# State-space layer on one Trainium2 core: the reads of its outputs move from the SP queue to the POOL queue

## The chip, the cores and the metric

The kernel runs on one core of one Trainium2 chip. The metric is device time in microseconds (us), the median of several executions; lower is better. The engines are TensorE (PE; its weight loads are listed as PEld), VectorE (DVE), ScalarE (ACT), GpSimd (POOL) and SyncE (SP). Each works through its own list of instructions in order, and waits on semaphores for the others and for transfers (DMAs). SP does nothing but issue DMAs. POOL issues DMAs too, and clears tiles between them.

## The reference, cut to what matters

The whole is a model of two blocks. The second block begins with a state-space layer, `s5_mixer`, on a sequence of 1024 positions and 1024 channels (64 groups of 16 channels, 64 states each):

```
bu_re = jnp.einsum('blgh,gph->lbgp', u, bb_re)
bu_im = jnp.einsum('blgh,gph->lbgp', u, bb_im)
_, _, s_re, s_im = lax.associative_scan(
    _ssm_combine, (a_seq_re, a_seq_im, bu_re, bu_im), axis=0)
y = (jnp.einsum('lbgp,ghp->blgh', s_re, c_re.astype(f32))
     - jnp.einsum('lbgp,ghp->blgh', s_im, c_im.astype(f32)))
y = y.reshape(bsz, seq, D_MODEL) + d_skip.astype(f32) * x.astype(f32)
h = jax.nn.gelu(y).astype(x.dtype)
val, gate = jnp.split(h @ w_glu, 2, axis=-1)
z = val * jax.nn.sigmoid(gate)
return (z @ w_out).astype(x.dtype)
```

## The kernel before

`block2` calls `s5_main`, which works in eight batches b = 0 to 7 of 128 channels (8 groups). The sequence is cut into 128 chunks of 8 positions. For one batch there are these steps, each a function inside `s5_main` or called by it:

- `s5_load(b)` and `u_tile(b)`: SP loads the tables E, ph, D and Co of the batch (five DMAs of 256 to 512 KB, L1476 and L1482) and the inputs U (eight DMAs of 64 KB, L1491). POOL first clears half of each of the two Co tiles (L1481).
- `states(b)`: PE multiplies U by E (tiles pe_re and pe_im, 32 matmuls, L1505). DVE turns the products by ph, scans over the chunks and turns back (L1247 to L1252 inside `cmul`, L1513); the result is S.
- `outputs(b)`: 48 matmuls on PE (tiles py, L1531 to L1533) from U, D, S and Co; ACT copies them to Y (L1534), and POOL writes Y to the scratch tensor y_d in HBM (tile name s5y, L1535, 512 KB).
- `tail(b)`: y_d is read back in another order, as eight DMAs of 64 KB (tile s5yt, L1544; one for each position within a chunk). ACT applies gelu (L1547) and casts the result (L215), DVE subtracts for the low halves (L216, tile s5hl, two of them).
- `glu(b)`: 12 matmuls on PE of s5hl with the first two weight panels (tile pg, L202 to L204).

The loop interleaves the batches:

```
for b in range(8):
    states(b)
    if b >= 1:
        outputs(b - 1)
        if b + 1 < 8:
            self.s5_load(b + 1)
            self.u_tile(b + 1)
    if b >= 3:
        tail(b - 3)
    if b >= 4:
        glu(b - 4)
```

After it come outputs(7), tail(5), glu(4), tail(6), and then glu(5) to glu(7) with the matmuls of two more panels (glu1, tile pg1) and tail(7) among them. The code's order is not the executed one: when the program is built, a scheduler of the tile framework sets the order of instructions on each engine, from its own estimate of when each is ready. So an edit of one line can change the order on engines that the line does not name. The order on every engine, once built, is fixed.

All tiles of 4 KB per partition share one pool of 40 buffers, so a load can have to wait until an older tile is no longer read. A DMA's completion is told on one of eight semaphores for the DMAs of SP and ACT, and one of eight others for those of POOL, taken in turn; a DMA waits for the one that used its semaphore before.

Of the kernel before, what the change touches and what calls it, by code (L numbers as in the profile page):

```python
# [103 lines left out]
class Core:  # L104
# [1388 lines left out]
    def s5_main(self):  # L1493
        nc, d = self.nc, self.d
        y_d = self.scr("s5y", [8, 8, 16, 8, P])
# [45 lines left out]
        def tail(b):  # L1541
            yt = self.t("s5yt", (P, 8, P))
            for t in range(8):
                nc.sync.dma_start(yt[:, t], y_d[b, t].rearrange("h g c -> g h c"))  # L1544
            yt = yt.rearrange("p s c -> p (s c)")
            y = self.t("s5y")
            nc.scalar.activation(y.rearrange("p (c s) -> p s c", s=8)[:, ::-1, ::-1],  # L1547
                                 yt.rearrange("p (s c) -> p s c", s=8), AF.Gelu_apprx_tanh)
            for hv, q in zip(HALVES, hs):
                hl = self.tr("s5hl", (P, 2, HB))  # L1550
                self.split(y[:, hv], hl[:, 0], hl[:, 1])
                q.append((hl[:, 0], hl[:, 1]))
            ys.append(y)
# [7 lines left out]
# [11 lines that stand above are left out]
        outputs(7)  # L1572
        tail(5)
        glu(4)
        tail(6)
        w1 = [self.weights(d["w_glu"][i], [P, KT, P], True) for i in (9, 1)]
        p1 = [self.psb("pg1") for _ in range(4)]
# [659 lines left out]
```

## Time and profile before

| what | value |
|---|---|
| median of 3 runs | 4070.12 us (4068.89 to 4072.51) |
| the profiled execution, its own time | 4067.31 us |
| its span, first to last instruction | 4065.5 us |
| PE busy, whole span | 3800.5 us (93%) |
| DVE busy | 2841.9 us (70%) |
| ACT busy | 1445.5 us (36%) |
| POOL busy | 308.7 us (8%) |
| granted TensorE clock, mean | 0.967 of full |

The page gives busy time by engine over the span, and the share says nothing of a single stage. Times in the answers of the trace count from the start of the span. The state-space layer's loop lies between about 1587 and 1707 us; the rows below are from there.

### The profile page before, as it was taken

To read this page: it belongs to the slowest core of one execution; us is meant where nothing else is said; L and a number is where in the kernel's file an instruction comes from. 1 tells how busy PE (TensorE), PEld (TensorE's weight loads), DVE (VectorE), ACT (ScalarE), POOL (GpSimd) and SP (SyncE) were. 2 spreads that over 40 slices of the span, in tenths; PEclk is the share of its full clock that TensorE was granted. 3 is DMA by queue.
4 is the path that set the end of the run, shared out by engine and by line. 5 is a ranking of instruction groups with operands and counts; after the bars stand their busy time and mean duration, and the time that the engine had idled before them with its cause. 6 is when DMAs were issued, how large, how long until landed. Compare 5 with 4: busy or idle time off the path is not lost.

```text
span 4065.5 us, 51267 instructions
## 1 busy us (share of the span) xinstructions
PE 3800.5 (93%) x19684; PEld 3145.8 (77%) x19684; DVE 2841.9 (70%) x4892; ACT 1445.5 (36%) x2328; POOL 308.7 (8%) x533
## 2 busy tenths in 40 slices
PE   7899899899999997799999999989999899999998
PEld 4778788778788866687788888878787677888886
DVE  5676767786888778667866664458878867666545
ACT  3222245533111221433423333335555634332332
POOL 0001100041010022000000000011010000000000
PEclk8999999999999998999999999989999899999999
DMA  6433321063222248513322245323232332122443
GB/s 235 138 113 128 111 77 42 28 212 130 73 73 74 98 148 253 164 53 103 125 80 76 94 153 171 122 83 99 73 99 73 89 124 109 73 94 78 170 159 111
DMA packets 172907, 458.35 MB, mean 113 GB/s; under 512 B 38542, under 2 KB 59028, under 8 KB 172662
## 3 DMA queue, kind: packets, MB, share of 16 engines
q1 hardware_dynamic: 129254, 317.94, 23.8%
q0 software_dynamic: 41104, 132.41, 9.9%
q10 hardware_dynamic: 2304, 4.72, 0.3%
q8 instruction: 155, 2.54, 0.3%
q14 instruction: 90, 0.74, 0.1%
HBM read 327.07 MB, written 100.66 MB: 105 GB/s over the span
## 4 chain that ended last, share of the span: by engine, by line
PE 75%; DVE 13%; issue 4%; DMA 3%; ACT 3%; POOL 1%; SPq 0%; POOLq 0%; DVEq 0%; ACTq 0%
PE p L202 7%; PE p L203 7%; PE p L204 7%; PE pd L202 4%; PE pd L204 4%; PE pd L203 4%; PE pout L202 2%; PE pout L204 2%; PE pout L203 2%; DVE sbm L1964 2%; PE pu L202 2%; PE pu L204 2%; PE pu L203 2%; PE pwt L1985 1%; PE pz L1047 1%
## 5 line engine op out<-in xcount | busy, mean ns | idle before, releaser
L185 DVE TENSOR_TENSOR wl<-wt,wh 128x1024 fp32r<-128x1024 f32 x232 | 283.3, 1222 | 276.5 <-ACT wh L184 274.1
L184 ACT CAST wh<-wt 128x1024 fp32r<-128x1024 f32 x232 | 242.9, 1048 | 653.5 <-PE pd L203 189.9
L202 PE MATMUL p<-tq,wq 128*128 128x512 f32 x736 | 290.5, 395 | 3.6 <-ACT wq L215 3.6
L203 PE MATMUL p<-tq,wq 128*128 128x512 f32 x736 | 290.0, 394 | 0.0
L204 PE MATMUL p<-tq,wq 128*128 128x512 f32 x736 | 290.0, 394 | 0.0
L202 PE MATMUL pd<-hd,wh 128*128 128x512 f32 x704 | 277.7, 394 | 2.8 <-DVE r L1831 2.8
L204 PE MATMUL pd<-hd,wl 128*128 128x512 f32 x704 | 276.5, 393 | 0.0
L203 PE MATMUL pd<-hd,wh 128*128 128x512 f32 x704 | 276.3, 393 | 0.0
L203 PE MATMUL p<-hq,wq 128*128 128x512 f32 x480 | 189.7, 395 | 0.0
L202 PE MATMUL p<-hq,wq 128*128 128x512 f32 x480 | 189.4, 395 | 0.0
L204 PE MATMUL p<-hq,wq 128*128 128x512 f32 x480 | 189.0, 394 | 0.0
L215 ACT CAST wq<-ws 128x512 fp32r<-128x512 f32 x184 | 114.3, 622 | 208.7 <-PE p L204 204.0
L1723 DVE TENSOR_TENSOR fsg<-fsg,p 128x512 f32<-128x512 f32 x140 | 94.4, 686 | 117.1 <-PE p L204 117.1
L202 PEld LDWEIGHTS p<-tq,wq 128*128 128x128 f32 x736 | 138.1, 188 | 43.3 <-ACT wq L215 4.9
L204 PEld LDWEIGHTS p<-tq,wq 128*128 128x128 f32 x736 | 138.3, 188 | 32.2
L203 PEld LDWEIGHTS p<-tq,wq 128*128 128x128 f32 x736 | 138.2, 188 | 30.6
L1723 DVE TENSOR_TENSOR fsu<-fsu,p 128x512 f32<-128x512 f32 x140 | 94.5, 687 | 93.7 <-PE p L204 93.6
L216 DVE TENSOR_TENSOR wq<-ws,wq 128x512 fp32r<-128x512 f32 x184 | 126.7, 690 | 46.4 <-ACT wq L215 44.5
L202 PEld LDWEIGHTS pd<-hd,wh 128*128 128x128 f32 x704 | 132.2, 188 | 33.9 <-DVE r L1831 4.2
L204 PEld LDWEIGHTS pd<-hd,wl 128*128 128x128 f32 x704 | 132.2, 188 | 31.2 <-DVE wl L185 0.6
L203 PEld LDWEIGHTS pd<-hd,wh 128*128 128x128 f32 x704 | 132.2, 188 | 30.0
L202 PE MATMUL pu<-hq,wh 128*128 128x512 f32 x320 | 129.8, 406 | 9.5 <-DVE cv L984 9.5
(702 smaller groups left out, 10657.4 us busy)
## 6 DMA issues: line engine op xcount, KB each, us to landing
wt<-w_gu SPq DMA_DIRECT2D x88, 512.0 KB
wt<-w_dn SPq DMA_DIRECT2D x88, 512.0 KB
wm<-w_mod SPq DMA_DIRECT2D x48, 512.0 KB
hid<-fsg POOLq DMA_DIRECT2D x44, 512.0 KB, 3.9
hr<-hid SPq DMA_DIRECT2D x44, 512.0 KB
wt<-w_od SPq DMA_DIRECT2D x28, 512.0 KB
khat<-fX POOLq DMA_DIRECT2D x24, 512.0 KB, 3.0
kh<-khat SPq DMA_DIRECT2D x24, 512.0 KB
```

Source lines behind the costliest of these rows:

```text
L184: nc.scalar.copy(wh, wt)
L185: nc.vector.tensor_tensor(wl, wt, wh.bitcast(F32), op=ALU.subtract)
L202: mm(ps, lh, rh, start=first, stop=False)
L203: mm(ps, lh, rl, start=False, stop=False)
L204: mm(ps, ll, rh, start=False, stop=last)
L215: self.nc.scalar.copy(h, src)
L216: self.nc.vector.tensor_tensor(l, src, h.bitcast(F32), op=ALU.subtract)
L1047: mm(p4[:, i, q], tb[:, m], z[:, self.POS[m]], start=True, stop=False)
L1723: add = lambda o, u, v: tt(o, u, v, op=ALU.add)
L1964: nc.vector.tensor_tensor_scan(om[:, :n - 1], om[:, :n - 1], self.inv[:, 3:4].to_broadcast([P, n - 1]), 1.0, op0=ALU.mult, op1=ALU.add)
L1985: nc.tensor.transpose(pt[:, s * P:(s + 1) * P], W[x][:, c:c + P], self.ident)
```

## The change

The eight DMAs of `tail` that read y_d back are issued by POOL instead of SP:

```diff
         def tail(b):
             yt = self.t("s5yt", (P, 8, P))
             for t in range(8):
-                nc.sync.dma_start(yt[:, t], y_d[b, t].rearrange("h g c -> g h c"))
+                nc.gpsimd.dma_start(yt[:, t], y_d[b, t].rearrange("h g c -> g h c"))
             yt = yt.rearrange("p s c -> p (s c)")
             y = self.t("s5y")
```

That is 64 DMAs in all. With it the built order changes on all engines. On SP the tail's reads are gone from between the loads. Before, where the inputs U of batch 4 have been issued (s5U_13155):

```order
L1491 DMA s5U_13155<-xf_d_11866 16x8x128 x8
L1544 DMA s5yt_13164<-s5y_12828 128x1x128 x8
L1476 DMA s5E_13253<-s5e_6947 128x1024
L1476 DMA s5ph_13255<-s5p_6949 128x1024
L1476 DMA s5D_13257<-s5m_6951 128x1024
```

and now:

```order
L1491 DMA s5U_13155<-xf_d_11866 16x8x128 x8
L1476 DMA s5E_13253<-s5e_6947 128x1024
L1476 DMA s5ph_13255<-s5p_6949 128x1024
L1476 DMA s5D_13257<-s5m_6951 128x1024
L1482 DMA s5Co_13259<-s5c_6948 64x1024
```

The loads of batch 5 (s5E_13253 and on) follow those of batch 4 at once.

On POOL the reads stand behind the write of a later batch. Tail 0 is s5yt_13164 and tail 1 is s5yt_13274; the Y tiles of batches 2, 3 and 4 are s5Y_13113, s5Y_13223 and s5Y_13345. Before:

```order
L1535 DMA s5y_12828<-s5Y_13113 128x1024
L1481 MEMSET s5Co_13152 64x1024
L1516 MEMSET s5S_13215 128x8
L1535 DMA s5y_12828<-s5Y_13223 128x1024
L1481 MEMSET s5Co_13259 64x1024
L1481 MEMSET s5Co_13262 64x1024
L1516 MEMSET s5S_13337 128x8
L1535 DMA s5y_12828<-s5Y_13345 128x1024
```

and now:

```order
L1535 DMA s5y_12828<-s5Y_13113 128x1024
L1481 MEMSET s5Co_13152 64x1024
L1544 DMA s5yt_13164<-s5y_12828 128x1x128 x8
L1516 MEMSET s5S_13215 128x8
L1481 MEMSET s5Co_13259 64x1024
L1535 DMA s5y_12828<-s5Y_13223 128x1024
L1481 MEMSET s5Co_13262 64x1024
L1544 DMA s5yt_13274<-s5y_12828 128x1x128 x8
L1516 MEMSET s5S_13337 128x8
```

So tail 1 is issued after the write of batch 3, and the same pattern goes on: tail k after the write of batch k + 2, up to tail 3.

On PE the twelve matmuls of glu 0 (tile pg0, from s5hl_13175 and s5hl_13178) move. Before, between the last matmul of batch 2's outputs (py5_13128) and the first of batch 3's (py5_13224), there stood only the states' products of batch 4:

```order
L1533 MATMUL py5_13128<-s5S_13012,s5Co_12966 128x128
L1505 MATMUL pe_re_13181<-s5U_13155,s5E_13143 64x128 x8
L1505 MATMUL pe_im_13182<-s5U_13155,s5E_13143 64x128 x8
L1531 MATMUL py5_13224<-s5U_13062,s5D_13054 128x128
L1532 MATMUL py5_13224<-s5S_13105,s5Co_13056 128x128
```

and now, at the same place, glu 0 comes first (its first rows):

```order
L1533 MATMUL py5_13128<-s5S_13012,s5Co_12966 128x128
L202 MATMUL pg0_12841<-s5hl_13175,wh_12831 128x512
L203 MATMUL pg0_12841<-s5hl_13175,wh_12831 128x512
L204 MATMUL pg0_12841<-s5hl_13175,wl_12832 128x512
L202 MATMUL pg0_12841<-s5hl_13178,wh_12831 128x512
```

and its last row is followed by what was next to py5_13128 before:

```order
L203 MATMUL pg0_12842<-s5hl_13178,wh_12837 128x512
L204 MATMUL pg0_12842<-s5hl_13178,wl_12838 128x512
L1505 MATMUL pe_re_13181<-s5U_13155,s5E_13143 64x128 x8
L1505 MATMUL pe_im_13182<-s5U_13155,s5E_13143 64x128 x8
L1531 MATMUL py5_13224<-s5U_13062,s5D_13054 128x128
```

Before, glu k stood behind the outputs of batch k + 3; now it stands ahead of the states' products of batch k + 4 and of those outputs. This holds for k = 0 to 3. Behind batch 7's outputs the order of PE is nearly the same as it was: glu 4, glu 5, then glu 6 and glu1.

## Rows read from the trace of the kernel before

**Rows 1.** The page, part 1: busy us, share of span, instructions.

```profile
PE 3800.5 (93%) x19684; PEld 3145.8 (77%) x19684; DVE 2841.9 (70%) x4892; ACT 1445.5 (36%) x2328; POOL 308.7 (8%) x533
```

**Rows 2.** Busy time by stretch, all engines; stretch, length, busy by engine, clock, DMA.

```profile
core 0: us, PE busy (x) PEld busy (x) DVE busy (x) ACT busy (x) POOL busy (x), PEclk, DMA share, GB/s
...
1630.00:1650.00 20.00, 14.60 (x126) 12.41 (x126) 11.17 (x23) 5.49 (x6) 2.48 (x4) 0.91 0.76 216
...
1690.00:1710.00 20.00, 13.24 (x74) 10.91 (x73) 11.10 (x22) 8.51 (x10) 0.53 (x1) 0.91 0.28 89
1710.00:1730.00 20.00, 20.00 (x88) 15.95 (x87) 17.73 (x28) 12.91 (x20) 0.00 (x0) 1.00 0.27 80
```

**Rows 3.** SP's queue in time: start, length, what, count.

```profile
1627.63 5.64 SPq L1544 DMA_DIRECT2D s5yt<-s5y  x8
...
1636.13 8.40 SPq L1491 DMA_DIRECT2D s5U<-xf_d  x8
1644.70 4.93 SPq L1544 DMA_DIRECT2D s5yt<-s5y  x8
...
1660.78 4.93 SPq L1544 DMA_DIRECT2D s5yt<-s5y  x8
...
1675.37 22.07 SPq L1544 DMA_DIRECT2D s5yt<-s5y  x32
```

**Rows 4.** ACT in time; the bracket is the idle time before, and who ended it.

```profile
1627.24 0.59 ACT L1534 COPY s5Y<-py 128x512 f32<-128x512 f32 x1 [2.09 <-PE py L1533]
...
1637.89 2.09 ACT L1547 ACTIVATE s5y<-s5yt 128x1024 f32<-128x1024 f32 x1
1640.02 1.14 ACT L215 CAST s5hl<-s5y 128x512 fp32r<-128x512 f32 x2
...
1652.77 2.12 ACT L1547 ACTIVATE s5y<-s5yt 128x1024 f32<-128x1024 f32 x1 [10.64 <-DVE s5w L1247]
...
1668.42 2.13 ACT L1547 ACTIVATE s5y<-s5yt 128x1024 f32<-128x1024 f32 x1 [10.57 <-DMA s5yt<-s5y]
...
1682.86 2.12 ACT L1547 ACTIVATE s5y<-s5yt 128x1024 f32<-128x1024 f32 x1 [8.41 <-DMA s5yt<-s5y]
```

**Rows 5.** Waits, stretch 1600 to 1740: who waited for whom, us, times, longest.

```profile
DVE s5hl L216 <- ACT s5hl L215: 21.2, 6, 7.2
```

**Rows 6.** Busy time of glu 0, then glu 1 (tile pg); columns PE, PEld, DVE, ACT.

```profile
1640.68:1646.21 5.53, 4.74 (x12) 3.23 (x12) 0.00 (x0) 0.00 (x0) 0.69 0.92 223
1656.98:1660.02 3.04, 3.03 (x12) 2.15 (x12) 0.00 (x0) 0.00 (x0) 1.00 1.09 215
```

**Rows 7.** The same for outputs 3 (tile py).

```profile
1631.87:1637.50 5.63, 5.62 (x48) 5.43 (x48) 0.00 (x0) 0.00 (x0) 1.00 0.77 248
```

**Rows 8.** The same, all engines, for the states' products of batch 5.

```profile
1647.63:1649.59 1.96, 1.96 (x33) 1.79 (x33) 1.96 (x5) 0.00 (x0) 0.00 (x0) 1.00 0.36 103
```

**Rows 9.** DVE in time: first and last product of states 4 behind pe_im.

```profile
1642.43 0.68 DVE L1248 TENSOR_TENSOR s5t<-pe_im,s5ph 128x512 f32<-128x512 f32 x1
...
1651.31 0.69 DVE L1252 TENSOR_TENSOR s5S<-s5S,s5t 128x508 f32<-128x508 f32 x1
```

**Rows 10.** POOL in time: the write of batch 2 and what follows.

```profile
1628.12 0.53 POOL L1535 DMA_DIRECT2D s5y<-s5Y  x1 [9.43 <-ACT s5Y L1534]
1628.69 0.95 POOL L1481 MEMSET s5Co<- 64x1024 f32 x1
```

**Rows 11.** POOL earlier in time: eight reads of HBM issued in a row.

```profile
1549.96 4.20 POOL L1419 DMA_DIRECT2D s5D<-s5g  x8
```

**Rows 12.** Line L1419, POOL's reads of 8 to 64 KB.

```profile
DMA to landing us min/median/max: 1.9/3.3/7.7
```

**Rows 13.** PE in time: from outputs 7 to glu 5.

```profile
1698.30 0.63 PE L1533 MATMUL py<-s5S,s5Co 128*128 128x128 f32 x2
...
1703.21 0.39 PE L1533 MATMUL py<-s5S,s5Co 128*128 128x128 f32 x2
...
1706.93 0.51 PE L202 MATMUL pg<-s5hl,wh 128*128 128x512 f32 x1 [1.71 <-ACT s5hl L215]
...
1710.14 0.40 PE L204 MATMUL pg<-s5hl,wl 128*128 128x512 f32 x1
```

## The prediction, as it stood before the changed kernel was run

> **What bounds the kernel now.** I read the shares of the page first [rows 1]: PE is busy 93% of the span, so most of the kernel is bounded by TensorE, but that is an average. The table of stretches comes next [rows 2]: between 1690 and 1710 us PE works 13.24 of 20 us at a clock of 0.91, and between 1630 and 1650 it works 14.60. So in the loop of the state-space layer PE waits, and something else sets the pace. From 1710 on it is busy 20.00 of 20 us at clock 1.00: what arrives earlier there gains nothing, and what delays the start of that stretch delays the end.
>
> The third view is SP's queue in time [rows 3]. The tails' reads cost SP 5.64, 4.93, 4.93 and 22.07 us, between loads, which take their turn behind them. That is the time the change frees. The fourth is ACT in time [rows 4]: the gelus of batches 0 to 3 start at 1637.89, 1652.77, 1668.42 and 1682.86, three turns in 44.97 us. Two of the three shown with their releaser waited for the tail's DMA, one for DVE. The waits [rows 5] say the rest: DVE's L216, which makes the low half of the gelu's result, waited 21.2 us in six times for ACT's L215, and behind it in DVE's list stand the products of the next states. So the tails are already near the path; how soon a tail lands matters.
>
> **What the change removes.** From SP, 64 issues: the 15.50 us of tails 0 to 2 between loads, and the 22.07 us of later ones, behind which no load of the loop stands. The loads of batch 5 begin at about 1627.6 instead of 1633.3. That gain reaches the end only if the loads are what the loop waits for afterwards; I come to that below.
>
> **What it adds.** POOL issues the 64. Eight such reads from HBM took POOL 4.20 us, 0.53 us each, when it did so earlier [rows 11]; 64 make 34 us on an engine busy 8% [rows 1]. As a share this is nothing. But POOL's list is fixed: tail k stands behind the write of Y(k+2) and a memset, and that write waits for ACT's copy, which waits for PE's outputs(k+2). Before, tail 0 stood on SP behind loads, and no outputs of a later batch were ahead of it in its list.
>
> **What it moves.** On PE, glu k goes ahead of the states' products of batch k+4 and of outputs(k+3). Each of these is harmless alone. Together they close a ring: tail k lands, gelu, the split, glu k, states' products, outputs(k+3), ACT's copy, the write of Y(k+3), tail k+1. No step of the ring can overlap another, and nothing in it can be walked past, since PE and POOL take their lists in order. I sum one turn from the rows:
>
> - gelu to the first matmul of glu: gelu 0 starts 1637.89 [rows 4], glu 0 at 1640.68 [rows 6]: 2.79 us.
> - glu: 5.53 us for glu 0, whose granted clock was 0.69, against 3.04 for glu 1 at 1.00 [rows 6]. I take 5.53, because PE idles in each turn of the ring before glu for longer than it did before glu 0 (3.18 us from the end of outputs 3 [rows 6, 7]), and glu 0, after that idle stretch, ran part of its time at the lower of the two levels (1.2 and 2.4 GHz).
> - states' products: 1.96 [rows 8]. Outputs(k+3): 5.63 [rows 7].
> - the last copy of Y begins at 1627.24 [rows 4], its write on POOL at 1628.12 [rows 10]: 0.88.
> - write and memset: from 1628.12 to 1628.69 + 0.95 = 1629.64 [rows 10]: 1.52.
> - eight issues; the last begins 3.67 us after the first (4.20 − 0.53) [rows 11].
> - landing of the last one: 3.3 us, the median of POOL's reads of 8 to 64 KB [rows 12]; 1.9 to 7.7 are the bounds. These are reads of HBM by the same queue and of about this size; the trace of before has no tail on POOL, so these are the nearest rows.
>
> The sum is 2.79 + 5.53 + 1.96 + 5.63 + 0.88 + 1.52 + 3.67 + 3.3 = 25.28 us; with glu at 3.04 and the landing at 1.9 it is 21.4, with the landing at 7.7 it is 29.7. Three turns are 75.9 us where they were 44.97: **+30.9** (+19.2 to +44.1).
>
> The start of the ring, tail 0: SP ended its issues at 1627.63 + 5.64 = 1633.27 [rows 3]; POOL would end at 1629.64 + 4.20 = 1633.84, which is +0.5, and I add 0.5 for landing beside SP's loads, which now run at the same time: **+1.0** (−0.3, if it lands a little sooner than SP's did, to +4, which is most of the way to the slow landing).
>
> The end of the ring: before, from gelu 3 (1682.86) to the start of glu 5 (1706.93) it is 24.07 us [rows 4, 13]. After, from gelu 3: 2.79 + 5.53 + 1.96, then DVE's work on states 7, first to last product 1642.43 to 1652.00 = 9.57 [rows 9], since outputs(7) need its S; 5.3 for what of outputs(7) follows S (1698.30 to 1703.60 [rows 13]); 0.9 to the write of Y(7); then POOL issues that write (0.53) and the last four reads of tail 5, which stand behind it, the last one some 2.1 us after the write begins; 3.3 for landing, 2.79 to glu 5. Sum 34.2: **+10.2** (+6.3 to +14.5, by the same bounds).
>
> Glu 5 itself: before it followed within 1.71 us and ran from 1706.93 to about 1710.5 [rows 13], some 3.45 us. After a longer wait I take glu 0's 5.53: **+2.1** (0 to +2.1). From there on PE is full [rows 2], and nothing later can swallow the delay.
>
> The sum: 30.9 + 1.0 + 10.2 + 2.1 = **+44.2** us; all lower ends together +25, all upper ends +65. What hides SP's freed time: the loads then come 5 us and more ahead of the ring, and the ring is longer than their period (16.1 us: from 1644.70 to 1660.78 on SP [rows 3]); so the whole of that gain lies idle on SP. Loads that come early only wait, also for buffers that the ring gives back late.
>
> On the landing a rule of the Trainium skill bears. The landing row for POOL's reads is a median of 3.3 us [rows 12]. The Trainium skill, "DMA: Bandwidth & Descriptors", section "Latency and other measured facts", puts the time to the first byte at about 1 us for GpSimd's path and about 0.6 for SP's and ACT's. An estimate by it: +0.4 for each of five tails, 2 us, and a sum of 46.2; no run here shows a first byte, and the row's median stands in my sum.
>
> **The rivals.** The first ends on the other side, faster. SP's freed issue time passes through: 5.64 + 4.93 + 4.93 = 15.5 us [rows 3] of the loop go, 4067.31 − 15.5 = 4051.8 in the profiled execution, 4054.6 on the median. It decides where the loads, not the tails, are what the next batch waits for, and where a tail lands before PE has come to glu k's new place, so that the ring never closes. For it speaks that the tails do stand ahead of loads on SP, and that POOL is idle. Against it: the gelus of batches 2 and 3 were ended by the tail's own DMA [rows 4], and after a write of Y(k+2) at least 1.52 + 3.67 + 1.9 + 2.79 = 9.9 us pass until glu k can start, while PE has no work in its list ahead of glu k but the rest of what it was doing. A rule of the same page, section "Issuing engines are not separate DMA queues", says that all issuing engines feed the same DMA engines and that issuing from several saves only issue time on the sequencers. By it this rival's gain is the 15.5 us of issue and no more, and the trace agrees in that those issues cost SP 4.93 us a tail.
>
> The second: about the same. If the tails, though later in POOL's list, land when they did (tail 0 within 1 us of before) and PE's wait for glu k is filled with what DVE needed anyway, as DVE also waited at L216 before [rows 5], then the period stays DVE's and ACT's, about 15 us, and the time stays within some 2 us of 4068 to 4070. Against it is the same ring: outputs(k+3) stood ahead of glu k before, and 5.63 + 0.88 + 1.52 us of the ring could then run beside the tail's landing.
>
> The third is slower still: POOL's reads land near their slow end, 7.7 us instead of 3.3, since 64 KB in rows of 512 bytes come in beside SP's loads, which are now bunched: 5 × 4.4 = 22 us more, about 4136.
>
> That the change doesn't move the reads at all is excluded: all 64 stand in POOL's list and none in SP's.
>
> **How the numbers follow.** The profiled execution took 4067.31, 2.81 below the median of 4070.12. With +44.2 it would be 4111.5; on the median that is 4114.3, and I forecast 4114. I give the ring 0.79, the slow landings 0.08, the faster rival 0.08, and no change 0.05. The range reaches from 4093, which is +23 (all lower ends together, +25, and 2 us more for an overlap that I do not see), to the slow landings, 4137. The faster rival and the case of no change stay outside, 0.13 of the chance, and some of the ring's own tails. Faster by over 0.2%, which is about what a measurement of this kernel can tell from no change, gets 0.08; within it 0.05; slower 0.87.
>
> **What would show it.** In the changed kernel's profile, ACT's gelus at L1547 should start some 25 us apart, not 15, and POOL's writes of Y too. PE should be idle ahead of the first matmul of each glu, ended by ACT's or DVE's halves of s5hl, with the states' products right behind glu. The tail's issues on POOL should take about 0.53 us each, and the last should land 3.3 us after its issue. SP should be idle between loads, or wait for buffers. Glu 5 should start near 1749 us instead of 1706.93, and from there to the end the two profiles should be alike, shifted. I am wrong if gelus come 15 or 16 us apart; if the landings on POOL are nearer to 2 us, or glu runs at full clock, the sum is too high by up to 4 us a turn; if DVE's own work, rather than the ring, releases PE, the term of the turn is wrong; and if an issue on POOL costs more than 0.53 us, eight of them a turn make it longer.

## The result, and the profile after

The changed kernel took 4123.03 us (median of 4 runs, 4121.83 to 4126.34) against 4071.32 beside it: a ratio of 1.0132, with an interval of 1.0117 to 1.0146. It is slower by 51.7 us. The forecast was 4114, in a range of 4093 to 4137. The profiled execution took 4121.83 us with a span of 4119.7, 54.2 more than the span before.

The table of stretches of the changed kernel, to be set against [rows 2] (stretch, length, busy by engine with counts, clock, DMA share, GB/s):

```profile
core 0: us, PE busy (x) PEld busy (x) DVE busy (x) ACT busy (x) POOL busy (x), PEclk, DMA share, GB/s
...
1630.00:1650.00 20.00, 0.24 (x3) 0.05 (x1) 4.23 (x8) 3.52 (x3) 7.25 (x12) 0.61 1.03 264
...
1690.00:1710.00 20.00, 8.21 (x44) 6.82 (x43) 8.88 (x19) 4.40 (x5) 7.25 (x12) 0.66 0.21 73
```

Where PE was busy for 14.60 us in 1630 to 1650, it is now busy for 0.24, and the DMA engines are full (1.03). Sixty us later PE is busy for 8.21 us, the clock is 0.66 and the DMA engines are nearly idle (0.21): nothing is short there, everything waits for one thing after another. That is the picture of a ring, and the first four gelus of ACT show its pace, where [rows 4] had 1637.89, 1652.77, 1668.42 and 1682.86:

```profile
1648.35 2.09 ACT L1547 ACTIVATE s5y<-s5yt 128x1024 f32<-128x1024 f32 x1
...
1678.01 2.09 ACT L1547 ACTIVATE s5y<-s5yt 128x1024 f32<-128x1024 f32 x1 [13.91 <-DMA s5yt<-s5y]
...
1702.62 2.09 ACT L1547 ACTIVATE s5y<-s5yt 128x1024 f32<-128x1024 f32 x1 [8.37 <-DMA s5yt<-s5y]
...
1726.84 2.09 ACT L1547 ACTIVATE s5y<-s5yt 128x1024 f32<-128x1024 f32 x1 [8.32 <-DMA s5yt<-s5y]
```

The turns are 29.66, 24.61 and 24.22 us, 78.49 in all, where they were 44.97. Each gelu after the first waits for its tail, as the brackets say. One turn can be walked on PE and POOL. PE, from glu 1 (the bracket is the idle time before, and who ended it):

```profile
1680.80 0.79 PE L202 MATMUL pg<-s5hl,wh 128*128 128x512 f32 x1 [17.32 <-ACT s5hl L215]
...
1685.78 0.40 PE L204 MATMUL pg<-s5hl,wl 128*128 128x512 f32 x1
1686.10 1.09 PE L1505 MATMUL pe_re<-s5U,s5E 128*64 128x128 f32 x16
...
1688.00 0.49 PE L1531 MATMUL py<-s5U,s5D 128*128 128x128 f32 x2
...
1693.24 0.39 PE L1533 MATMUL py<-s5S,s5Co 128*128 128x128 f32 x2
```

PE stood for 17.32 us, all of it for the split of tail 1; then glu, the states' products and the outputs followed each other without a gap. POOL, around tail 0 and then where the walk goes on (start, length, what, count):

```profile
1631.16 0.53 POOL L1535 DMA_DIRECT2D s5y<-s5Y  x1 [10.23 <-ACT s5Y L1534]
...
1632.62 4.17 POOL L1544 DMA_DIRECT2D s5yt<-s5y  x7
1640.48 0.59 POOL L1544 DMA_DIRECT2D s5yt<-s5y  x1 [3.68 <-DMA s5Co<-s5c]
...
1694.55 0.59 POOL L1535 DMA_DIRECT2D s5y<-s5Y  x1 [22.80 <-ACT s5Y L1534]
1695.18 0.94 POOL L1481 MEMSET s5Co<- 64x1024 f32 x1
1696.07 4.70 POOL L1544 DMA_DIRECT2D s5yt<-s5y  x8
```

The write of Y(4) at 1694.55 waits for ACT's copy, and the eight reads stand behind it. They end at 1700.8, the last lands, and gelu 2 starts at 1702.62: the ring is closed. The other thing to see is tail 0: its eighth read waited 3.68 us. The landing of the reads themselves, for tails 0, 1 and 2 (count, duration of an issue in ns min/median/max, first and last start; then us from issue to landing):

```profile
L1544 POOL DMA_DIRECT2D s5yt<-s5y x8: 587/620/645, 1632.6 to 1640.5; - x8
...
DMA to landing us min/median/max: 6.5/8.6/8.9
...
L1544 POOL DMA_DIRECT2D s5yt<-s5y x8: 595/621/662, 1665.9 to 1670.0; - x8
...
DMA to landing us min/median/max: 2.3/7.9/8.5
...
L1544 POOL DMA_DIRECT2D s5yt<-s5y x8: 595/621/662, 1696.1 to 1700.1; - x8
...
DMA to landing us min/median/max: 2.2/2.4/2.4
```

Most reads of tails 0 and 1 landed some 8 us after their issue (medians 8.6 and 7.9), those of tail 2 after 2.4 (tail 3: 2.3). Two rows of SP's queue say what was in flight at the first two:

```profile
1632.60 10.22 SPq L1491 DMA_DIRECT2D s5U<-xf_d  x8
...
1666.85 0.34 SPq L1476 DMA_DIRECT2D s5E<-s5e  x1
```

SP issued the loads of batch 5 from 1629.69 to 1642.82, over tail 0, and those of the last batch from 1666.85 on, over tail 1. Behind that there were no loads over a tail.

How much the stage itself grew is read between two landmarks, POOL's eight reads ahead of it ([rows 11], 1549.96 before) and ACT's table load behind it. In the changed kernel the reads, and then the table load in the kernel before and in the changed one:

```profile
1552.78 4.15 POOL L1419 DMA_DIRECT2D s5D<-s5g  x8
```

```profile
1734.74 1.28 ACT L1611 ACT_TABLE_LOAD   x1
```

```profile
1791.54 1.28 ACT L1611 ACT_TABLE_LOAD   x1
```

From one to the other it was 184.78 us and is 238.76: the stage is 54.0 us longer.

### The profile page after: what moved, and what is told of

It is laid out like the page before. It is cut to its first block, busy times and chain, and to the rows that moved or that the text cites. A ratio compares the mean times of both kernels' runs of the same rounds, so it can differ in the third digit from the quotient of the medians.

```text
span 4119.7 us, 51296 instructions
## 1 busy us (share of the span) xinstructions
PE 3812.1 (93%) x19684; PEld 3156.1 (77%) x19684; DVE 2842.2 (69%) x4892; ACT 1445.3 (35%) x2328; POOL 345.9 (8%) x597
## 4 chain that ended last, share of the span: by engine, by line
PE 74%; DVE 13%; issue 6%; ACT 3%; DMA 3%; POOL 1%; SPq 0%; POOLq 0%; DVEq 0%; ACTq 0%
PE p L202 7%; PE p L204 7%; PE p L203 7%; PE pd L202 4%; PE pd L203 4%; PE pd L204 4%; DVE sbm L1964 2%; PE pout L202 2%; PE pout L204 2%; PE pout L203 2%; PE pu L202 2%; PE pu L204 2%; PE pu L203 2%; PE pwt L1985 1%; PE pz L1047 1%
## 5 line engine op out<-in xcount | busy, mean ns | idle before, releaser
L203 PEld LDWEIGHTS p<-tq,wq 128*128 128x128 f32 x736 | 138.8, 189 | 30.9
L202 PEld LDWEIGHTS pd<-hd,wh 128*128 128x128 f32 x704 | 132.2, 188 | 34.2 <-DVE r L1831 4.2
```

The source lines that it names most:

```text
L202: mm(ps, lh, rh, start=first, stop=False)
L203: mm(ps, lh, rl, start=False, stop=False)
```

## The experiments

Twelve kernels were run. All times are medians, all ratios are against the kernel before on the same chip; the recorded ratios differ by up to 0.0008, some 3 us, from the quotients of the medians, so that smaller differences say nothing. Of the edits the essential part is shown; `...` stands for what is left out. In most of them an order in an engine's list is held by hand: what is traced under `issue_after(x)` stands behind x in the list of x's engine, without a wait.

### Is it a ring? Cut it at PE, at POOL, at both, or make the order on PE alone

The ring theory says that two edges are needed: glu k ahead of outputs(k+3) on PE, and tail k+1 behind the write of Y(k+3) on POOL. Four kernels take the edges apart. The first holds glu k behind outputs(k+3), with the tails on POOL:

```diff
+                self.last = nc.cur_bb.bb.instructions[-1]
                 nc.scalar.copy(Y[:, hb::2], py.rearrange("p (g c) -> p g c", g=4))
...
             if b >= 4:
-                glu(b - 4)
+                with self.tc.issue_after(self.last):
+                    glu(b - 4)
```

> The tails stay on POOL, each behind the write of Y(k+2), but on PE glu k is held behind outputs(k+3), as it stood before the change. The ring theory: the ring is cut at PE; what remains is gelu k, ACT's copies of Y(k+3), the write and tail k+1, some 13 us, below DVE's own pace, so the turns go back to about 15 us. The late start of tail 0 (7.6 us in the changed kernel) and a few us at the end stay: 4072 to 4092, 4082 as the middle. Rival, tails on POOL are slow by themselves (their place behind the writes, or their landing): the gelus stay 24 us apart or more and the time stays at 4115 to 4125.

It took 4077.42 us, ratio 1.0024 (1.0012 to 1.0036). Its gelus:

```profile
1648.74 2.09 ACT L1548 ACTIVATE s5y<-s5yt 128x1024 f32<-128x1024 f32 x1
1661.31 2.13 ACT L1548 ACTIVATE s5y<-s5yt 128x1024 f32<-128x1024 f32 x1 [8.34 <-DMA s5yt<-s5y]
1678.64 2.11 ACT L1548 ACTIVATE s5y<-s5yt 128x1024 f32<-128x1024 f32 x1 [8.39 <-DMA s5yt<-s5y]
1691.25 2.13 ACT L1548 ACTIVATE s5y<-s5yt 128x1024 f32<-128x1024 f32 x1 [8.36 <-DMA s5yt<-s5y]
```

Tail 0 is as late as in the changed kernel (1648.74), but the three turns take 42.51 us, even less than before. ACT still stands idle for 8.4 us ahead of a gelu, until its tail has landed, but PE's outputs no longer wait for that.

The second makes the order on PE alone, with all tails on SP:

```diff
         for b in range(8):
-            states(b)
+            if b >= 4:
+                glu(b - 4)
+                with self.tc.issue_after(nc.cur_bb.bb.instructions[-1]):
+                    states(b)
+            else:
+                states(b)
...
-            if b >= 4:
-                glu(b - 4)
```

> The tails are on SP, in SP's order of before; on PE glu k goes ahead of the states' products of batch k+4 and of outputs(k+3), as in the changed kernel. The ring theory: the order on PE alone closes no ring, since SP issues a tail without waiting for a write of Y. It adds a serial piece in each turn on DVE: split 1.3, glu cold 5.5, products 1, states 9.6, so 17.4 us a turn instead of 15: 4073 to 4095, 4080 as the middle. Rival, the order on PE does it all: gelus about 25 us apart and 4110 to 4125.

It took 4083.7 us, ratio 1.0038 (1.0023 to 1.0053). DVE in time, over one turn:

```profile
1669.67 0.69 DVE L1247 TENSOR_TENSOR s5w<-pe_re,s5ph 128x512 f32<-128x512 f32 x1 [5.40 <-PE pe_re L1505]
...
1679.42 0.69 DVE L1252 TENSOR_TENSOR s5S<-s5S,s5t 128x508 f32<-128x508 f32 x1
1680.02 1.28 DVE L216 TENSOR_TENSOR s5hl<-s5y,s5hl 128x512 fp32r<-128x512 f32 x2
```

DVE now paces it: states, split, then 5.4 us for glu and the products, 17.05 us a turn (the split follows at 1662.98, 1680.02 and 1697.09). So the order on PE by itself costs about 2 us a turn, as summed, and not 10. The rest of what it costs lies at the end: from gelu 3 (1693.62) to glu 5 (1724.85) it is 31.2 us, where it was 24.1.

The third keeps the order on PE of the changed kernel, and puts tail k ahead of the write of Y(k+2) on POOL:

```diff
-            nc.gpsimd.dma_start(y_d[b].rearrange("t h g c -> (t h) g c"), Y)
+            if 2 <= b < 7:
+                tail(b - 2)
+                with self.tc.issue_after(self.ltail):
+                    nc.gpsimd.dma_start(y_d[b].rearrange("t h g c -> (t h) g c"), Y)
+            else:
+                nc.gpsimd.dma_start(y_d[b].rearrange("t h g c -> (t h) g c"), Y)
...
+            self.ltail = nc.cur_bb.bb.instructions[-1]
...
-            if b >= 3:
-                tail(b - 3)
```

> The tails are on POOL, but tail k stands ahead of the write of Y(k+2) in POOL's list, behind that of Y(k+1); PE has the order of the changed kernel. The ring theory: the ring now goes over two batches, 25 us for two turns, so it no longer binds; the serial piece on DVE of 17.4 us a turn does: 4068 to 4092, 4078 as the middle. Rival, POOL's reads land late by themselves or the order on PE does it all: 4110 to 4125.

It took 4078.82 us, ratio 1.0013 (0.9996 to 1.003). Its gelus start at 1633.72, 1649.85, 1666.77 and 1683.76, 17 us apart after the first turn, the same pace of DVE as in the second kernel. The fourth has both edits, that of the first kernel and that of the third:

> Both cuts: tail k ahead of the write of Y(k+2) on POOL, and glu k behind outputs(k+3) on PE. The ring theory: nothing ties a tail to the outputs of a later batch, SP's freed time can pass through, and the turns come down to DVE's work and the loads' pace, 12 to 15 us: 4050 to 4072, 4062 as the middle. Rival, POOL's reads are slow by themselves: above 4080.

It took 4059.54 us, ratio 0.9977 (0.9968 to 0.9986), the first version that is faster than the kernel before. Between the two landmarks, though, its profile is only 0.9 us shorter than that of the kernel before (183.92 for 184.78); the rest of its lead arises behind the stage, and no trace here shows from what. PE's waits in it, and then its table of stretches:

```profile
1631.75 1.98 PE L1505 MATMUL pe_re<-s5U,s5E 128*64 128x128 f32 x16 [6.24 <-DMA s5U<-xf_d]
...
1676.88 1.97 PE L1505 MATMUL pe_re<-s5U,s5E 128*64 128x128 f32 x16 [6.24 <-DMA s5U<-xf_d]
...
1703.30 0.79 PE L202 MATMUL pg<-s5hl,wh 128*128 128x512 f32 x1 [5.32 <-ACT s5hl L215]
```

```profile
1630.00:1650.00 20.00, 14.37 (x124) 13.09 (x124) 14.07 (x27) 9.00 (x9) 11.34 (x20) 0.84 1.00 276
1650.00:1670.00 20.00, 18.84 (x152) 17.41 (x151) 18.43 (x38) 5.64 (x7) 8.37 (x14) 0.96 1.02 247
```

Now PE waits for the inputs U, and the DMA engines are full from 1610 to 1670 (1.01, 1.00 and 1.02), where before they were at 0.76 to 0.93. The tails had been in the loads' way, and with them gone the transfers themselves are.

What follows: each of the first three kernels is without 39 to 46 of the 51.7 us, so neither POOL as the issuer nor the order on PE is dear by itself. Between the landmarks the stage grew by 13.6, 13.0 and 13.1 us in them, and by 54.0 with both edges: of the 54.0, 13.6 come with the tails on POOL alone and 13.0 with the order on PE alone, and 27.4 are there only when both meet. That is shown by the runs and not only argued.

### Why tail 0 came late

One kernel gives tail 0 alone back to SP, with the changed kernel's order on PE held by hand (left out here):

```diff
-                nc.gpsimd.dma_start(yt[:, t], y_d[b, t].rearrange("h g c -> g h c"))
+                (nc.sync if b == 0 else nc.gpsimd).dma_start(yt[:, t], y_d[b, t].rearrange("h g c -> g h c"))
...
```

> The changed kernel, with tail 0 alone issued by SP again (at its place of before, ahead of the loads of batch 5); the order on PE and that of the other tails on POOL are the changed kernel's. Theory: tail 0 came 7.6 us late on POOL, because its last read waited for the write of Y(2), whose landing had grown from 3.5 to 9.0 us beside SP's loads, and then landed late too; on SP it comes about when it did before. The ring starts 6 to 9 us earlier and is otherwise as long: 4110 to 4119, 4115 as the middle. Rival, the lateness came from the stage's earlier part or is made up by the next turn: 4120 to 4126.

It took 4112.34 us, ratio 1.0106 (1.0091 to 1.0121), 10.7 below the changed kernel. Its first two gelus:

```profile
1641.73 2.09 ACT L1547 ACTIVATE s5y<-s5yt 128x1024 f32<-128x1024 f32 x1
1672.62 2.08 ACT L1547 ACTIVATE s5y<-s5yt 128x1024 f32<-128x1024 f32 x1 [13.89 <-DMA s5yt<-s5y]
```

The ring starts 6.6 us earlier, and its turns are 30.89, 25.13 and 24.76 us, 2.3 longer in all. That leaves 4.3 of gain, and the profiled execution took 4117.82, 4.0 below that of the changed kernel; it was the slowest of the four, and for the rest of the median's 10.7 no trace shows a reason. Another kernel leaves out the loads of batches 5 to 7 instead, with the orders on PE and POOL held as in the changed kernel (left out here):

```diff
-                if b + 1 < 8:
+                if b + 1 < 5:
                     self.s5_load(b + 1)
                     self.u_tile(b + 1)
+                    kept = dict(st[b + 1]), self.U[b + 1]
+                elif b + 1 < 8:
+                    st[b + 1], self.U[b + 1] = dict(kept[0]), kept[1]
...
```

> The changed kernel with the loads of batches 5 to 7 left out (they reuse the tables and inputs of batch 4), the orders on PE and POOL held as in the changed kernel; the clearing of two Co tiles ahead of a tail goes with them. Theory: the slow landings of tails 0 and 1 (8 to 9 us instead of 2.3) come from SP's loads in flight; without them turn 1 falls from 29.7 to about 24, tail 0 comes some 5 us earlier, and each turn loses the memset's 0.9: 10 to 17 us off, 4106 to 4114. The ring itself stays, some 23.5 us a turn. Rival, the first reads on POOL land late for another reason: 4118 to 4124.

It took 4107.96 us, ratio 1.0092 (1.0073 to 1.011); the clearing of the Co tiles goes with the loads. Gelus 0 and 1:

```profile
1638.68 2.09 ACT L1548 ACTIVATE s5y<-s5yt 128x1024 f32<-128x1024 f32 x1
1662.37 2.09 ACT L1548 ACTIVATE s5y<-s5yt 128x1024 f32<-128x1024 f32 x1 [7.22 <-DMA s5yt<-s5y]
```

and the landing of tail 0's reads, from the view of that line:

```profile
L1545 POOL DMA_DIRECT2D s5yt<-s5y x8: 595/626/653, 1630.7 to 1634.9; - x8
...
DMA to landing us min/median/max: 2.2/2.4/2.5
```

Without SP's loads, tail 0 has no wait between its reads, they land in 2.4 us instead of 8.6, and the first turn is 23.69 us instead of 29.66. The ring itself stays: the next two turns are 24.11 and 24.12. The slow landings come from SP's loads in flight, not from POOL's queue. The wait ahead of the eighth read is a wait for the write of Y(2): POOL's DMAs take eight semaphores in turn, and that write used the one which the eighth read takes. It landed 9.0 us after its issue at 1631.16, that is at 1640.2, just ahead of 1640.48; before, it took 3.5, and without the late loads 2.9. The row names a load of Co, but in the kernel with halved reads (below) the same wait names the write.

### Is the ring in all of it? The last four tails back on SP, and smaller reads

One kernel gives tails 4 to 7 back to SP and leaves 0 to 3 on POOL:

```diff
-                nc.gpsimd.dma_start(yt[:, t], y_d[b, t].rearrange("h g c -> g h c"))
+                (nc.gpsimd if b < 4 else nc.sync).dma_start(yt[:, t], y_d[b, t].rearrange("h g c -> g h c"))
```

> The changed kernel, with tails 4 to 7 issued by SP again and tails 0 to 3 on POOL. Theory: the three turns of the ring stay, and of the end term goes what came from tail 5's last four reads behind the write of Y(7): PE's wait of 6.2 us ahead of glu 5 and the cold start of glu 5, 2 us, in all about 8: 4110 to 4119, 4114 as the middle. Rival A, the end is set by the states and outputs of batch 7: 4120 to 4126. Rival B, the ring is made by the later tails: below 4095.

It took 4117.49 us, ratio 1.0118 (1.01 to 1.0137). Ahead of glu 5, where PE waited 6.20 us in the changed kernel:

```profile
1757.94 0.72 PE L202 MATMUL pg<-s5hl,wh 128*128 128x512 f32 x2 [0.62 <-ACT s5hl L215]
```

The end's wait is gone, as expected, and from gelu 3 (1728.53) to glu 5 it is 29.4 us instead of 34.6. The three turns grew by 1.9 us (to 80.38): SP now issues reads of tails 4 and 5 meanwhile (from 1697.89 on), and POOL's reads of tails 2 and 3 take up to 3.2 and 3.4 us to land, where they took up to 2.4 and 2.5. On the medians 5.5 us are left of the 8 that I expected. Rival B falls: the ring is in tails 0 to 3.

Another splits each tail into 16 reads of 32 KB, with the order on PE held (left out here):

```diff
-                nc.gpsimd.dma_start(yt[:, t], y_d[b, t].rearrange("h g c -> g h c"))
+                for g in range(0, 8, 4):
+                    nc.gpsimd.dma_start(yt[16 * g:16 * g + 64, t], y_d[b, t].rearrange("h g c -> g h c")[g:g + 4])
...
```

> The changed kernel with each tail's reads split in two, 16 of 32 KB instead of 8 of 64 KB, the order on PE held as in the changed kernel. Theory: the issues lie on the ring, 0.58 us each as measured in the changed kernel, so a turn grows by 8 x 0.58 = 4.6 us: three turns 14, tail 0 up to 4.6, the end 4 to 6 (thirteen reads of tail 5 instead of four now stand behind the write of Y(7)): 4138 to 4156, 4146 as the middle. Rival, the issues run beside the landing and the turn is set by the landing of the whole 512 KB: 4118 to 4130.

It took 4161.15 us, ratio 1.0223 (1.0208 to 1.0238), 38 us above the changed kernel and above my upper end. The turns were 33.42, 30.26 and 28.87 us, 14.06 more in all, where 14 were expected: issues on the ring are paid in full. What I had sized wrongly stands at both ends. Gelu 0 came at 1661.72, 13.4 us later than in the changed kernel. POOL at tail 0:

```profile
1645.22 0.61 POOL L1545 DMA_DIRECT2D s5yt<-s5y  x1 [4.32 <-DMA s5y<-s5Y]
1646.21 4.80 POOL L1545 DMA_DIRECT2D s5yt<-s5y  x8 [0.38 <-DMA s5yt<-s5y]
```

The eighth read waits for the write of Y(2), now by name, and eight more stand behind it. And at the end, the reads of tails 5 to 7 that stand behind the write of Y(7) are 45 now, 27.06 us of POOL's time without a gap, for which glu 5 and glu 6 waited 11.25 and 3.58 us.

The same split, in the kernel with both cuts:

> The kernel with both cuts (tail k ahead of the write of Y(k+2) on POOL, glu k behind outputs(k+3) on PE), and each tail's reads split in two, 16 of 32 KB. The same 64 more issues cost the changed kernel 38 us. Ring theory: off the ring the issues run beside other work and cost little, since POOL has room: 4056 to 4070, 4062 as the middle, against 4059.5 without the split. Rival, smaller reads are dear wherever they stand (more transfers beside SP's loads): above 4080.

It took 4086.72 us, ratio 1.0045 (1.003 to 1.006), 27 us above the same kernel without the split. My expectation is wrong here, and the rival named in it, above 4080, came true. One stretch and PE's two waits in it:

```profile
1710.00:1730.00 20.00, 6.65 (x14) 4.14 (x15) 2.23 (x4) 6.91 (x7) 20.00 (x34) 0.64 0.20 56
```

```profile
1719.42 0.80 PE L202 MATMUL pg<-s5hl,wh 128*128 128x512 f32 x1 [11.34 <-ACT s5hl L215]
...
1729.08 0.62 PE L202 MATMUL pg<-s5hl,wh 128*128 128x512 f32 x1 [3.81 <-ACT s5hl L215]
```

POOL is busy for 20.00 of 20 us: the last tails are a plain queue of issues at 0.6 us each, and PE waits for them. That is 15.2 us, against 5.3 in the kernel without the split, some 10 of the 27. In the loop, gelus 1 and 2 came 14.1 and 16.7 us later, and gelus 3 and 4 still 10; POOL's reads wait there for landings of earlier ones, again in SP's loads. That makes some 20. Between the landmarks the two profiles differ by 24.0 us; what makes the other 4, and the 3 behind the stage, stays open. So sixty-four further issues are dear off the ring too, and of the 38 us that they cost the changed kernel only the 14 of its turns are the ring's.

### A version that beats both

In the kernel with both cuts PE waited for U. Here SP issues U ahead of the tables:

```diff
-                    self.s5_load(b + 1)
                     self.u_tile(b + 1)
+                    self.s5_load(b + 1)
```

> The kernel with both cuts, and in each batch SP issues the inputs U ahead of the tables E, ph, D and Co. With both cuts PE waited for U's loads four times, 17.5 us in all, so the loads bound the loop then. If that is what binds, U first gives part of it back: 4044 to 4058, 4052 as the middle. Rival, the loads as a whole are late and PE waits for E or D instead: 4056 to 4064, no change.

It took 4061.24 us, ratio 0.9975 (0.9965 to 0.9984): no change against 4059.54 without it. PE's waits moved from U to the tables and to DVE, which is the rival: the loads as a whole are late, with the DMA engines full. The same edit in the kernel before:

> The kernel before (tails on SP), with U issued ahead of E, ph, D and Co in each batch; the scheduler then puts the two halves of glu k in another order too. It says how much of the gain of U first is its own. Where the tails pace the loop, as the trace of before shows, nothing much moves: 4062 to 4074. Rival, U's loads bounded the loop before too: 4045 to 4060.

4069.2 us, ratio 1.0001 (0.999 to 1.0013), as expected nothing. Last, tails 5 to 7 of the kernel with both cuts go back to SP:

```diff
-                nc.gpsimd.dma_start(yt[:, t], y_d[b, t].rearrange("h g c -> g h c"))
+                (nc.gpsimd if b < 5 else nc.sync).dma_start(yt[:, t], y_d[b, t].rearrange("h g c -> g h c"))
```

> The kernel with both cuts, and tails 5 to 7 issued by SP, which has no loads of the loop left by then. With both cuts PE had no gap from 1677 us on, so an earlier tail 5 gains nothing: 4056 to 4064. Rival, the last tails on POOL still hold the end: 4048 to 4056.

4057.77 us, ratio 0.9973 (0.996 to 0.9987): within the interval of 4059.54. My reason was wrong, though. PE did have a gap of 5.32 us ahead of glu 5 in the kernel with both cuts (the row above), and this edit took it away (0.60 us are left); but gelus 0 to 4 came 3 to 6 us later in this execution, of which 2.3 were there ahead of the stage, so that glu 5 started at 1703.09 instead of 1703.30. Whether the rest is the edit or the execution, one profile cannot say. The kernel with both cuts is the best that is clear: 0.23% faster than before and 1.5% faster than the changed one, with all reads on POOL.

## Why the prediction was right, and where it was off

**The mechanism** was right, and so was the size to 7.5 us: 44.2 forecast, 51.7 measured on the medians. In the profiled execution the terms are these.

**The ring's turn**, forecast at 25.28. The second turn is 24.61, and its steps can be laid beside the sum: gelu to glu 1680.80 − 1678.01 = 2.79 (2.79 forecast), glu 5.30 (5.53), products 1.90 (1.96), outputs to ACT's last copy 5.66 (5.63), copy to write 0.89 (0.88), write to the first read 1.52 (1.52), first read to the last 4.04 (3.67), landing 2.4 (3.3). Two were off, in opposite directions: an issue on POOL took 0.58 us from start to start, not 0.53, which makes +0.4, and a read with no load of SP in flight landed in 2.4 us, which makes −0.9. Glu ran cold, as forecast, but that its size fits is in part luck: of the 5.53 us taken from glu 0 before, PE was busy for 4.74 [rows 6], and the rest was a wait for the split's low half:

```profile
1641.96 0.80 PE L203 MATMUL pg<-s5hl,wh 128*128 128x512 f32 x1 [0.78 <-DVE s5hl L216]
```

In the changed kernel that wait is gone and the clock is lower than the 0.69 of [rows 6]. The table of stretches of glu 1 and glu 5 in the changed kernel, beside [rows 6] (columns PE, PEld, DVE, ACT):

```profile
1680.80:1686.10 5.30, 5.30 (x12) 3.62 (x12) 0.00 (x0) 0.00 (x0) 0.55 0.20 49
1761.41:1767.05 5.64, 5.64 (x12) 4.13 (x13) 0.00 (x0) 0.00 (x0) 0.50 0.33 109
```

PE had stood for 17.32 and 6.20 us ahead of them, and the granted clock in them was 0.55 and 0.50, the lower of the two levels (1.2 GHz) for nearly all of it. The three turns made +33.5 where +30.9 was forecast; the excess is the first turn, 29.66, whose reads met SP's loads.

**Tail 0** is the term that was mis-sized: +1.0, with +4 as the upper end. Gelu 0 came 10.46 us later. Of that, 2.82 were there already before the stage (POOL's eight reads of [rows 11], at 1549.96 before, stand at 1552.78 in the changed kernel's trace) and are not the change's. (In the other kernels these reads start anywhere from 1548.09 to 1556.07.) The rest, 7.6, is. I had allowed 0.5 us for landing beside SP's loads, which came from no row, and had written the slow landing of 7.7 us off as a rival for all tails alike. It happened, for the two tails that SP's loads could meet. And I had not seen that the write of Y(2) would share the slow landing and hold the eighth read through its semaphore, though the description of the kernel above has all of it: eight semaphores in turn, and the eighth read behind a write takes that write's.

**The end**, from gelu 3 to glu 5: 1761.41 − 1726.84 = 34.57, forecast 34.2, so +10.5 for +10.2. Here too parts cancel: glu 3 took 4.82 us for 5.53, and from the products' end (1736.35) to the last copy of Y(7) (1752.48) it was 16.13 for 14.87. **Glu 5** cold: 5.64 − 3.45 = +2.2 for +2.1. The sum of the four is 7.6 + 33.5 + 10.5 + 2.2 = 53.8, against 54.0 between the landmarks. That the spans differ by nearly the same, 54.2, is chance: the changed kernel's execution was 2.8 us behind ahead of the stage and made up 2.6 after it, mostly past 2700 us, where every other profiled kernel gains 0.8 to 3.0 us on this execution of the kernel before.

**The freed time of SP**: I said that it would lie idle on SP. It did (SP issues no load between 1656 and 1666.85), but it also did harm, since the loads that came early came on top of tail 0. With both cuts no ring swallows it, and still the first rival's 15.5 us do not come through: SP's three last groups of U reads took 12.66, 9.92 and 11.37 us of its queue there, where they took 8.40, 8.16 and 6.73 before, so that the last of them ended at 1672.94 instead of 1675.21. The median is 11.5 us below the kernel before, but how much of that is SP's freed time, no run separates. The Trainium skill, "DMA: Bandwidth & Descriptors", section "Issuing engines are not separate DMA queues", says that what SP and POOL issue ends on the same DMA engines and interleaves there. These traces agree: POOL's reads took 2.4 us without SP's loads and some 8 beside them, and with both cuts the DMA share stood at 1.0.

**The rivals.** Faster did not come about, because of both edges; with both cut the time is 0.23% below the kernel before, which is less than the 15.5 us. About the same needed the old order on PE: with it the time was 4077, so it was near, but not the change's. Slower still, by slow landings, came true for two tails of eight.

## What to carry to other kernels

Moving a DMA to an idle queue moves it behind everything that stands ahead of it there, and an idle engine's list can be the one that waits for the bottleneck. Read the whole built order after such an edit, on the engines that were not named too, and look for a cycle: a transfer that stands behind the result of the work that waits for the transfer before it. If there is one, its period is the plain sum of its steps; here a cut at either of the two edges gave most of it back.

## What the runs showed of the hardware that I had not expected

The landing of a 64 KB read issued by POOL went from 2.4 us with no load of SP in flight to some 8 to 9 beside SP's loads, and that of a 512 KB write, the one of Y(2), from 3.5 in the kernel before and 2.9 without the late loads to 9.0. An issue on POOL took 0.58 us in a row of eight, and 45 issues in a row took 27.06 us in the kernel with halved reads, during which PE waited. With both cuts and halved reads POOL is busy for 9% of the span (385.0 us), and for 20.00 of 20 us where it mattered.
